# A whole fp32 copy of two kept products beside their high and low parts, in a hybrid recurrent and attention layer

## The chip, the cores and the metric

The kernel runs on one core of a Trainium2 chip. The metric is the time of the whole program on that core in microseconds (us), smaller is better. Engines are named as in the profile: PE multiplies matrices, DVE and ACT are the vector and the scalar engine, SP issues the transfers, POOL does next to nothing here.

## What is computed

One decoder layer over 2048 tokens of 1024 features, all in fp32. What matters here is its middle: the tokens attend to 256 fixed memory tokens in four heads. The reference, cut to that:

```python
h = rms_norm(x, xa_norm_g[l])
m = rms_norm(mem, mem_norm_g[l])
q = (h @ w_q[l]).reshape(bsz, s, XA_HEADS, XA_HD)
k, v = jnp.split(m @ w_kv[l], 2, axis=-1)
scores = jnp.einsum("bshd,bmhd->bhsm", q, k) * (XA_HD ** -0.5)
p = jax.nn.softmax(scores, axis=-1)
o = jnp.einsum("bhsm,bmhd->bshd", p, v).reshape(bsz, s, d)
x = x + o @ w_o[l]
```

Ahead of it stands a mixer (a gated linear recurrence beside a convolution module with 31 taps, one input and one output projection), behind it a gated feed-forward part with a short convolution, and a last norm.

## The kernel before

**Two parts per operand.** PE multiplies rounded fp32 (`fp32r`). To keep precision each operand is split into a high part `h` (ACT copies it with rounding) and a low part `l` (DVE subtracts the high part from the source); a product is three matmuls: high by high, high by low, low by high (`mm3`).

**Folded attention weights.** Since memory and weights are fixed over the tokens, the kernel first makes two weights from them: `A`, 1024 by 1024, which takes normed tokens straight to scores (from the keys and `w_q`), and `VO`, which takes probabilities straight to the output (from the values and `w_o`). `memory_a` makes `A`: 16 banks of PSUM of 128 by 512, each with two blocks of 128 by 256. `memory_vo` makes `VO`: 16 banks of 128 by 512. Each bank is split into a pair (`ah`, `al`, or `voh`, `vol`), and `keep` stores both parts to DRAM (tensors `A2`, `VO2`), from where they are fetched again whenever they are used.

**Tokens in four groups of 512.** Groups 0 and 1 go through the attention one after the other. Groups 2 and 3 go as a pair, by Strassen's scheme with seven products for eight. For it `Folds.prepare` makes four combinations (`T1` to `T4`) of the blocks of each weight: `w_out`, `A` and `VO`. It takes every block through `Folds.block`: that of `w_out` is fetched whole from the input; for `A` and `VO` both parts are fetched and DVE adds them (`wd<-wh,wl`). That is 16 blocks for `A` and 16 for `VO`. The combinations go to DRAM and are split when they are used. The feed-forward part follows in two halves and takes the last 1,400 us or so.

**Order of the work.** The code writes tasks (mixers `m`, attentions `a`, `mem_a`, `mem_vo`, `fold` and others) which are stepped by a clock of PE's planned work. The instructions that they write are then put in order by a list scheduler (`Program.schedule`): each has a due time that follows from the place of its users on PE, an estimated duration and an engine, and each engine takes the one due first of those that are ready; 84 slots of 128 by 512 fp32 in SBUF and 8 banks of PSUM are given out in the order of the program. The schedule fixes the order on each engine, and the tile framework adds the semaphores. All instructions are thus recorded at line 399, which is why the profile is read by tiles. All large transfers go through one queue, SP's, in order.

**Names.** `raw` is a weight as fetched, `wh`/`wl` its parts; `mt` the normed memory, `kvh`/`kvl` keys or values, `qth`/`qtl` the turned `w_q`; `x` a token tile, turned on PE by products with the identity (`ps<-ident,x`) and split to `xh`/`xl`; `cb`, `conv` the 31-tap convolution, whose 30 steps are DVE's `conv<-cb,v,conv`; `hid` and `X` operands of the feed-forward part.

Of the kernel before, what the change touches and what calls it, by code (L numbers as in the profile page):

```python
# [11 lines left out]
F32 = mybir.dt.float32  # L12
F32R = mybir.dt.float32r
AF = mybir.ActivationFunctionType
ALU = mybir.AluOpType
# [407 lines left out]
def hybrid_layer(  # L423
# [17 lines left out]
    pr = Program(nc, place)  # L441
# [4 lines left out]
    def V(name, *a, **k):  # L446
        pr.do("DVE", name, *a, **k)

    def ACT(out, in_, func, **k):
        pr.do("ACT", "activation", out, in_, func, **k)  # L450
# [4 lines left out]
    def transpose(o, in_, idn):  # L455
        pr.do("PE", "transpose", o, in_, idn)
# [8 lines left out]
    def ps():  # L465
        return pr.new("ps", name="ps")

    def tmp(name="tmp"):
        return pr.new("S", name=name)

    def rnd(name, shape=None):
        return pr.new("S", shape, F32R, name)

    def pair(name, shape=None):
        return rnd(name + "h", shape), rnd(name + "l", shape)
# [48 lines left out]
    def small(w):  # L524
        at = n_small[0]
        n_small[0] += w
        return Buf(None, (P, w), smalls[:, at : at + w])
# [49 lines left out]
    def split(src, hi, lo):  # L577
        ACT(hi[:], src, AF.Copy)
        V("tensor_tensor", lo[:], src, hi[:].f32(), op=ALU.subtract)
# [26 lines left out]
    class Kept:  # L606


        def __init__(self, name, n, dtype=F32R):
            self.t = drp.tile([n * P, TT], F32, name=name)  # L610
            self.tok = {}
            self.dtype, self.name, self.n = dtype, name, n
# [9 lines left out]
        def get(self, i, shape=None, name=None):  # L622
            b = pr.new("S", shape, self.dtype, name or self.name)
            pr.dma((b[:] if shape is None else flat(b)).f32(), self.at(i), reads=[self.tok[i]])
            return b
# [6 lines left out]
    def raw_rows(w, r0):  # L632
        st = pr.new("W", (P, D), name="raw")
        pr.dma(st[:], w[r0 : r0 + P, :])
        return st
# [41 lines left out]
    class Rows:  # L677


        def __init__(self, w, name, n, uses):  # L680
            self.w, self.kept, self.uses, self.seen = w, Kept(name, n * 4), uses, {}

        def get(self, k, half):
            base = (k * 2 + half) * 2
# [240 lines left out]
    def kv(c0):  # L925

        hi, lo = pair("kv")
        pp = [ps(), ps()]
        for kq in range(2):
            st = raw_cols(w_kv[0], c0, kq)  # L930
            for f in range(2):
                with together():
                    for k in range(KQ):
                        sl = slice((k % 2) * M, (k % 2 + 1) * M)
                        matmul(pp[f][:, :M], st[:, k, f * P : (f + 1) * P], mt[kq * 2 + k // 2][:, sl], start=kq + k == 0, stop=kq == 1 and k == KQ - 1)
            yield 0
        for f in range(2):
            fs = slice(f * M, (f + 1) * M)
            ACT(hi[:, fs], pp[f][:, :M], AF.Copy)
            V("tensor_tensor", lo[:, fs], pp[f][:, :M], hi[:, fs].f32(), op=ALU.subtract)  # L940
        return hi, lo

    def keep(rows, k, half, cols, src):

        base = (k * 2 + half) * 2
        for i in range(2):
            tok = rows.kept.tok.setdefault(base + i, Buf(None, (1,)))
            pr.dma(rows.kept.at(base + i)[:, cols], src[i].f32(), writes=[tok], join=True)

    def memory_a():  # L950
        pr.first = True
        xs = []
        for mb in range(2):
            parts = []
            ssp = small(2)
            for half in range(2):
                t = tmp("mem")
                pr.dma(t[:], mem[0, mb * P : (mb + 1) * P, half * TT : (half + 1) * TT])
                ACT(junk[:], t[:], AF.Square, accum_out=ssp[:, half : half + 1])
                parts.append(t)  # L960
            r = small(1)
            V("tensor_tensor", r[:], ssp[:, 0:1], ssp[:, 1:2], op=ALU.add)
            ACT(r[:], r[:], AF.Sqrt, bias=eps[:], scale=1.0 / D)
            V("reciprocal", r[:], r[:])
            for t in parts:
                ACT(t[:], t[:], AF.Copy, scale=r[:, 0:1])
            xs.append(parts)
        for k2 in range(NK // 2):
            t = tmp("mt")
            p = ps()  # L970
            with together():
                for kk in range(2):
                    k = 2 * k2 + kk
                    for mb in range(2):
                        transpose(p[:, kk * M + mb * P : kk * M + (mb + 1) * P], xs[mb][k // 4][:, (k % 4) * P : (k % 4 + 1) * P], ident[:])
            for kk in range(2):
                sl = slice(kk * M, (kk + 1) * M)
                ACT(t[:, sl], p[:, sl], AF.Copy, scale=vec["v1024"][:, 2 * k2 + kk, G_MEM : G_MEM + 1])
            mt.append(t)
        pr.first = False  # L980
        yield MEM_WAIT
        def operands(h):
            kk = yield from kv(h * M)
            yield 0

            qt = []
            for kq in range(2):
                st = raw_cols(w_q[0], h * M, kq)
                for db in range(2):
                    p = ps()  # L990
                    with together():
                        for j in range(KQ):
                            transpose(p[:, j * P : (j + 1) * P], st[:, j, db * P : (db + 1) * P], ident[:])
                    hi, lo = pair("qt")
                    split(p[:], hi, lo)
                    qt.append((hi, lo))
            yield 1
            return kk, qt

        nxt = yield from operands(0)  # L1000
        for h in range(4):
            (kh, kl), qt = nxt
            if h < 3:
                nxt = yield from operands(h + 1)
            for k2 in range(NK // 2):
                p = ps()
                with together():
                    for kk in range(2):
                        k = 2 * k2 + kk
                        for db in range(2):  # L1010
                            hi, lo = qt[(k // KQ) * 2 + db]
                            cs = slice((k % KQ) * P, (k % KQ + 1) * P)
                            ks = slice(db * M, (db + 1) * M)
                            mm3(p[:, kk * M : (kk + 1) * M], hi[:, cs], lo[:, cs], kh[:, ks], kl[:, ks], db == 0, db == 1)
                t = pair("a")
                split(p[:], *t)
                for kk in range(2):
                    keep(A_rows, 2 * k2 + kk, h // 2, slice((h % 2) * M, (h % 2 + 1) * M), [b[:, kk * M : (kk + 1) * M] for b in t])
                yield 0
            yield 0  # L1020

    def memory_vo():
        yield mem_a
        yield VO_LATE
        for h in range(4):
            vh, vl = yield from kv(D + h * M)
            yield 1
            pp = [ps() for _ in range(4)]
            for db in range(2):
                st = raw_rows(w_o[0], h * M + db * P)  # L1030
                ww = []
                for half in range(2):
                    hi, lo = pair("w")
                    split(st[:, half * TT : (half + 1) * TT], hi, lo)
                    ww.append((hi, lo))
                for i, p in enumerate(pp):
                    mb, (wh, wl) = i // 2, ww[i % 2]
                    vs = slice(db * M + mb * P, db * M + (mb + 1) * P)
                    with together():
                        mm3(p[:], vh[:, vs], vl[:, vs], wh[:], wl[:], db == 0, db == 1)  # L1040
                    if i % 2:
                        yield 0
            for i, p in enumerate(pp):
                t = pair("vo")
                split(p[:], *t)
                keep(VO_rows, h * 2 + i // 2, i % 2, slice(0, TT), [b[:] for b in t])


# [589 lines left out]
    class Folds:  # L1638
# [5 lines left out]
        def block(self, k, half):  # L1644
            if self.rows.w is not None:
                t = tmp("wd")
                pr.dma(t[:], self.rows.w[k * P : (k + 1) * P, half * TT : (half + 1) * TT])
                return t
            hi, lo = self.rows.get(k, half)
            t = tmp("wd")  # L1650
            V("tensor_tensor", t[:], hi[:].f32(), lo[:].f32(), op=ALU.add)
            return t

        def prepare(self, wait):
            for i in range(KH):
# [348 lines left out]
    m, n, a = mixers, normeds, attends  # L2004
# [44 lines left out]
```

## Time and profile before

| | us |
|---|---|
| median of three runs | 2402.87 |
| lowest and highest run | 2400.91, 2404.35 |
| the profiled execution, its own time | 2401.64 |
| its span in the trace | 2399.8 |
| PE, DVE, ACT busy in it | 2385.4, 2034.9, 1319.6 |

The granted clock of PE was 0.999 over the span. 604.56 MB were moved by DMA, 252 GB/s on average. PE's rows overlap: a matmul of 128 by 512 is shown with some 390 ns, and the next one starts 226 to 227 ns later. So a share of busy time says only that PE never stopped; where it waits is read from the waits and from the distance of starts. The same holds in a lesser degree for DVE and ACT, whose rows overlap by about 0.1 us. In the trace an fp32 product that is not rounded (`ps<-mt,raw`) has two rows where the program has one instruction.

### The profile page before, as it was taken

The page shows a single profiled execution, that of the slowest core. Times are in us where ns is not written, and L with a number is a line of the kernel's source. Part 1 is how long each engine was busy: PE and PEld are TensorE (multiplying, and loading weights), DVE is VectorE, ACT ScalarE, POOL GpSimd, SP SyncE. Part 2 cuts the span into 40 slices and gives each one's busy share as a digit, 9 for nine tenths or more (in the row PEclk, how much of TensorE's full clock was granted, in tenths as well). Part 3 has the DMA queues.
Part 4 walks back from the last instruction along what each step waited for, and adds up shares of the span by engine and source line. Part 5 has one row for each costly group of instructions (what it writes and reads, how often), then busy time and mean ns, then how long its engine had stood idle before and what let it go on. Part 6 is the DMA issues. An engine that isn't in the chain of part 4 may idle for free.

```text
span 2399.8 us, 33427 instructions
## 1 busy us (share of the span) xinstructions
PE 2385.4 (99%) x10940; PEld 1977.0 (82%) x10940; DVE 2034.9 (85%) x3353; ACT 1319.6 (55%) x2380; POOL 0.7 (0%) x6
## 2 busy tenths in 40 slices
PE   9999999999999999999999999999999999999998
PEld 8798888888887888888888888888888888888887
DVE  6999995299899869879999887988988896777787
ACT  7782676357557778695555555554555541222333
POOL 0000000000000000000000000000000000000000
PEclk9999999999999999999999999999999999999999
DMA  9688788775878988787766544556565599887986
GB/s 308 220 297 314 241 298 301 255 263 175 289 261 272 322 275 273 277 284 268 253 231 205 199 171 158 174 177 211 192 215 199 184 308 321 283 280 253 315 299 255
DMA packets 364434, 604.56 MB, mean 252 GB/s; under 512 B 35371, under 2 KB 117547, under 8 KB 364260
## 3 DMA queue, kind: packets, MB, share of 16 engines
q1 hardware_dynamic: 364108, 602.16, 73.3%
q8 instruction: 86, 1.41, 0.2%
q14 instruction: 88, 0.72, 0.1%
q10 hardware_dynamic: 152, 0.28, 0.0%
HBM read 409.36 MB, written 192.94 MB: 251 GB/s over the span
## 4 chain that ended last, share of the span: by engine, by line
PE 84%; DVE 9%; ACT 3%; DMA 2%; issue 1%; SPq 0%; DVEq 0%; ACTq 0%
PE ps L399 84%; DVE conv L399 4%; DMA h<-hid 1%; DMA wl<-w_down 1%; ACT L399 1%; DVE wl L399 1%; DVE hidl L399 0%; DVE s L399 0%; DVE acc L399 0%; ACT gate L399 0%; DVE al L399 0%; ACT junk L399 0%; DMA wl<-w_in 0%; DVE xc L399 0%; DVE xl L399 0%
## 5 line engine op out<-in xcount | busy, mean ns | idle before, releaser
L399 PE MATMUL ps<-Xh,wh 128*128 128x512 f32 x1344 | 523.5, 390 | 0.7 <-ACT u L399 0.7
L399 PE MATMUL ps<-Xh,wl 128*128 128x512 f32 x1344 | 523.4, 389 | 0.7 <-DVE wl L399 0.5
L399 PE MATMUL ps<-Xl,wh 128*128 128x512 f32 x1344 | 523.2, 389 | 0.0
L399 PE MATMUL ps<-wh,hidl 128*128 128x512 f32 x960 | 374.4, 390 | 1.0 <-DVE hidl L399 1.0
L399 PE MATMUL ps<-wh,hidh 128*128 128x512 f32 x960 | 374.5, 390 | 0.8 <-ACT hidh L399 0.8
L399 PE MATMUL ps<-wl,hidh 128*128 128x512 f32 x960 | 373.8, 389 | 0.0
L399 DVE SCALAR_TENSOR_TENSOR conv<-cb,v,conv 128x512 f32<-128x512 f32 x480 | 337.1, 755 | 2.2 <-ACT conv L399 1.4
L399 PEld LDWEIGHTS ps<-Xh,wl 128*128 128x128 f32 x1344 | 252.4, 188 | 53.6 <-DVE wl L399 1.5
L399 PEld LDWEIGHTS ps<-Xh,wh 128*128 128x128 f32 x1344 | 252.4, 188 | 53.1 <-ACT u L399 1.1
L399 PEld LDWEIGHTS ps<-Xl,wh 128*128 128x128 f32 x1344 | 252.4, 188 | 52.4
L399 ACT ACTIVATE hidh<-s 128x512 fp32r<-128x512 f32 x186 | 113.8, 631 | 271.1 <-DVE s L399 232.6
L399 PEld LDWEIGHTS ps<-wh,hidl 128*128 128x128 f32 x960 | 180.3, 188 | 40.2 <-DVE hidl L399 3.1
L399 PEld LDWEIGHTS ps<-wh,hidh 128*128 128x128 f32 x960 | 180.3, 188 | 38.3 <-ACT hidh L399 1.3
L399 PEld LDWEIGHTS ps<-wl,hidh 128*128 128x128 f32 x960 | 180.3, 188 | 37.1
L399 PE MATMUL ps<-xh,wh 128*128 128x512 f32 x512 | 204.6, 400 | 0.5 <-DVE vol L399 0.5
L399 PE MATMUL ps<-xh,wl 128*128 128x512 f32 x512 | 200.4, 391 | 0.0
L399 PE MATMUL ps<-xl,wh 128*128 128x512 f32 x512 | 200.1, 391 | 0.0
L399 ACT ACTIVATE wh<-s 128x512 fp32r<-128x512 f32 x192 | 119.5, 629 | 116.7 <-DVE s L399 82.0
L399 ACT ACTIVATE wh<-raw 128x512 fp32r<-128x512 f32 (+2 forms) x214 | 127.9, 613 | 54.2 <-PE ps L399 22.7
L399 ACT ACTIVATE u<-ps 128x512 f32<-128x512 f32 x144 | 85.7, 595 | 129.1 <-PE ps L399 128.2
L399 DVE TENSOR_TENSOR wl<-raw,wh 128x512 fp32r<-128x512 f32 (+2 forms) x214 | 141.5, 675 | 14.7 <-ACT wh L399 13.7
L399 DVE TENSOR_TENSOR acc<-acc,ps 128x512 f32<-128x512 f32 (+1 forms) x157 | 103.4, 682 | 59.2 <-PE ps L399 55.3
(241 smaller groups left out, 4029.9 us busy)
## 6 DMA issues: line engine op xcount, KB each, us to landing
raw<-in_w_up_dram SPq DMA_DIRECT2D x96, 512.0 KB
wh<-w_down SPq DMA_DIRECT2D x156, 256.0 KB
wl<-w_down SPq DMA_DIRECT2D x156, 256.0 KB
w_down<-wh SPq DMA_DIRECT2D x144, 256.0 KB
w_down<-wl SPq DMA_DIRECT2D x144, 256.0 KB
h<-hid SPq DMA_DIRECT2D x120, 256.0 KB
wh<-w_in SPq DMA_DIRECT2D x96, 256.0 KB
wl<-w_in SPq DMA_DIRECT2D x96, 256.0 KB
```

The source lines that it names most:

```text
L399: getattr(e, name)(*[resolve(a) for a in args], **{k: resolve(a) for k, a in kw.items()})
```

## The change

A third tensor of whole fp32 values is kept for `A` and for `VO` (`A2w`, `VO2w`). `split_kept` makes it: after the split ACT copies the same bank of PSUM once more, unrounded, to a tile `aw` or `vow`, and `keep` stores that too. `Folds.block` then fetches the whole block instead of both parts, and DVE's addition is gone.

```diff
         def __init__(self, w, name, n, uses):
             self.w, self.kept, self.uses, self.seen = w, Kept(name, n * 4), uses, {}
+            self.whole = None if w is not None else Kept(name + "w", n * 2, F32)
...
             pr.dma(rows.kept.at(base + i)[:, cols], src[i].f32(), writes=[tok], join=True)
+        tok = rows.whole.tok.setdefault(k * 2 + half, Buf(None, (1,)))
+        pr.dma(rows.whole.at(k * 2 + half)[:, cols], src[2], writes=[tok], join=True)
+
+    def split_kept(name, p):
+        t = *pair(name), tmp(name + "w")
+        split(p[:], *t[:2])
+        ACT(t[2][:], p[:], AF.Copy)
+        return t
...
-                t = pair("a")
-                split(p[:], *t)
+                t = split_kept("a", p)
...
-                t = pair("vo")
-                split(p[:], *t)
+                t = split_kept("vo", p)
...
-            hi, lo = self.rows.get(k, half)
-            t = tmp("wd")
-            V("tensor_tensor", t[:], hi[:].f32(), lo[:].f32(), op=ALU.add)
-            return t
+            return self.rows.whole.get(k * 2 + half, None, "wd")
```

In numbers of instructions: ACT has 16 `aw<-ps` and 16 `vow<-ps` more and three loads of its function tables fewer (81 to 78); DVE has 32 `wd<-wh,wl` fewer; SP has 32 stores `A2w<-aw` of 128 KB and 16 stores `VO2w<-vow` of 256 KB more, 32 fetches `wd` of 256 KB more, and 64 fetches of parts fewer. PE's instructions are the same 10,790. The scheduler puts the rest in a new order. PE's first difference is its 690th instruction, and from about its 4,520th on, which is all of the feed-forward part, its order is as before. On DVE, ACT and SP the order differs in pieces between about 120 and 1,200 us of the trace of before, and hardly after that.

Three places show what moved. The first is PE at the end of `memory_a`, where the second group of tokens is turned and its mixer begins. Before:

```order
L399 MATMUL ps<-mt,raw 128x256 x8
L399 MATMUL ps<-ident,x 128x128 x24
L399 MATMUL ps<-mt,raw 128x256 x4
L399 MATMUL ps<-ident,x 128x128 x8
L399 MATMUL ps<-xh,wh 128x512
L399 MATMUL ps<-xl,wh 128x512
L399 MATMUL ps<-xh,wl 128x512
```

Now:

```order
L399 MATMUL ps<-mt,raw 128x256 x8
L399 MATMUL ps<-ident,x 128x128 x16
L399 MATMUL ps<-mt,raw 128x256 x4
L399 MATMUL ps<-ident,x 128x128 x4
L399 MATMUL ps<-mt,raw 128x256 x4
L399 MATMUL ps<-ident,x 128x128 x12
L399 MATMUL ps<-wh,kvh 128x512
L399 MATMUL ps<-wl,kvh 128x512
L399 MATMUL ps<-wh,kvl 128x512
```

Four more products for the values (`ps<-mt,raw`) and then the first 24 products for `VO` now stand between the turned tokens and the mixer's first product; before, they stood among the mixer's products.

The second place is DVE over the same stretch, from the last subtractions of `A` on. Before:

```order
L399 TENSOR_TENSOR al<-ps,ah 128x512
L399 TENSOR_TENSOR wl<-raw,wh 128x512 x2
L399 SCALAR_TENSOR_TENSOR conv<-cb,v_99,conv 128x512
L399 TENSOR_TENSOR wl<-raw,wh 128x512 x2
L399 SCALAR_TENSOR_TENSOR xl<-ps,v_98,xh 128x512 x5
L399 TENSOR_TENSOR kvl<-ps,kvh 128x256
L399 SCALAR_TENSOR_TENSOR xl<-ps,v_98,xh 128x512 x3
```

Now:

```order
L399 SCALAR_TENSOR_TENSOR conv<-cb,v_101,conv 128x512 x3
L399 TENSOR_TENSOR smalls<-smalls 128x4
L399 SCALAR_TENSOR_TENSOR conv<-cb,v_101,conv 128x512 x2
L399 RECIPROCAL smalls<-smalls 128x4
L399 TENSOR_TENSOR al<-ps,ah 128x512 x2
L399 SCALAR_TENSOR_TENSOR conv<-cb,v_101,conv 128x512 x9
L399 SCALAR_TENSOR_TENSOR xl<-ps,v_100,xh 128x512 x2
L399 TENSOR_TENSOR wl<-raw,wh 128x512 x2
L399 TENSOR_TENSOR kvl<-ps,kvh 128x256
L399 TENSOR_TENSOR wl<-raw,wh 128x512
L399 SCALAR_TENSOR_TENSOR xl<-ps,v_100,xh 128x512
```

Nine steps of the convolution now stand between the last `al` and the first `xl`, where one stood, and the sums of the tokens' norm (`smalls`) stand shortly ahead of the last `al` instead of ahead of the last head. Between the first and the last `al` there are three more steps of the convolution than before (30 to 27), and 68 instructions in all to 65.

The third is ACT at the last head of `A`, with the engines that each row waits for. Before:

```order
L399 ACTIVATE x<-x,smalls 128x512
L399 ACTIVATE ah<-ps 128x512 [waits PE_49]
L399 ACTIVATE x<-x,smalls 128x512
L399 ACTIVATE x<-x,smalls 128x512 [waits DMAHW4_49]
L399 ACTIVATE ah<-ps 128x512 [waits PE_49]
```

Now:

```order
L399 ACTIVATE aw<-ps 128x512 [waits DVE_49]
L399 ACTIVATE ah<-ps 128x512 [waits PE_49]
L399 ACTIVATE smalls<-smalls,eps 128x4 [waits DVE_49]
L399 ACTIVATE aw<-ps 128x512
L399 ACTIVATE ah<-ps 128x512 [waits PE_49]
L399 ACTIVATE aw<-ps 128x512
L399 ACTIVATE x<-x,smalls 128x512 [waits DVE_49]
L399 ACTIVATE x<-x,smalls 128x512 x6
L399 ACTIVATE x<-x,smalls 128x512 [waits Activation_49]
```

Before, the eight token tiles were scaled (`x<-x,smalls`) among the copies of `A`; now all eight stand behind the last of them. Six of the 16 `aw` rows wait for DVE.

## The prediction

> **What bounds the kernel now.** I read the page first, then PE's waits, then the stretches.
>
> ```profile
> span 2399.8 us, 33427 instructions
> PE 2385.4 (99%) x10940; PEld 1977.0 (82%) x10940; DVE 2034.9 (85%) x3353; ACT 1319.6 (55%) x2380; POOL 0.7 (0%) x6
> PE 84%; DVE 9%; ACT 3%; DMA 2%; issue 1%; SPq 0%; DVEq 0%; ACTq 0%
> ```
>
> PE is busy in all but 14.4 us, and the chain that ended last is PE's for 84%. A change that leaves PE's work alone can give back only its waits. These are all that the view of waits lists for PE:
>
> ```profile
> PE ps L399 <- DMA raw<-in_w_in_dram: 1.6, 1, 1.6
> PE ps L399 <- POOL ident masks.py:199: 1.4, 1, 1.4
> PE ps L399 <- DVE hidl L399: 1.0, 2, 0.6
> PE ps L399 <- DVE xl L399: 0.8, 2, 0.5
> PE ps L399 <- ACT hidh L399: 0.8, 1, 0.8
> PE ps L399 <- ACT u L399: 0.7, 1, 0.7
> PE ps L399 <- DVE wl L399: 0.5, 1, 0.5
> PE ps L399 <- DVE vol L399: 0.5, 1, 0.5
> PE ps L399 <- ACT prob L399: 0.3, 1, 0.3
> ```
>
> The first two are the start, `xl` is there before the change sets in, and `hidl`, `hidh`, `u` and `wl` (3.0 us) lie behind 1,000 us, in the feed-forward part. In the stretch that is reordered only `vol` and `prob` remain, 0.8 us. In the chain told in order of time PE runs alone over long pieces:
>
> ```profile
> 265.09 450.67 PE ps L399 x2109
> 770.20 722.32 PE ps L399 x3302
> ```
>
> DVE's share lies ahead of the first, below 265 us, and between 716 and 770. There DVE hardly rests (columns: length; busy time and rows of PE, PEld, DVE, ACT, POOL; clock, DMA share, GB/s):
>
> ```profile
> 120.00:140.00 20.00, 20.00 (x123) 18.47 (x122) 19.97 (x34) 19.85 (x35) 0.00 (x0) 1.00 0.80 261
> 140.00:160.00 20.00, 20.00 (x144) 19.00 (x144) 20.00 (x35) 14.65 (x37) 0.00 (x0) 1.00 0.93 317
> 160.00:180.00 20.00, 20.00 (x139) 18.42 (x138) 20.00 (x34) 15.88 (x29) 0.00 (x0) 1.00 0.97 313
> 180.00:200.00 20.00, 20.00 (x90) 16.66 (x89) 19.54 (x30) 4.52 (x8) 0.00 (x0) 1.00 0.85 281
> 200.00:220.00 20.00, 20.00 (x91) 16.89 (x91) 19.86 (x32) 6.23 (x13) 0.00 (x0) 1.00 1.05 395
> 680.00:720.00 40.00, 40.00 (x180) 32.09 (x179) 39.48 (x64) 24.59 (x35) 0.00 (x0) 1.00 0.82 278
> 720.00:760.00 40.00, 39.74 (x195) 32.14 (x194) 39.55 (x65) 36.89 (x66) 0.00 (x0) 1.00 0.80 273
> ```
>
> From 120 to 180 us, where `A` is made, PE and DVE are full, DMA nearly, and ACT has 9.6 us left of 60. That is where the change adds. Where it removes, PE has next to no waits.
>
> **What it removes.** The additions, by the view of the tile `wd`:
>
> ```profile
> L399 DVE TENSOR_TENSOR wd<-wh,wl x32: 671/688/702, 611.4 to 965.8; 128x512 f32<-128x512 f32 x32
> ```
>
> 32 x 0.688 = 22.0 us of DVE, and 32 fetches of 256 KB (8.4 MB) out of that stretch. DVE is full in part of it (39.55 of 40 above), but PE's waits there sum to 0.3 us (`prob`). So 22 us of DVE are worth 0.3 us at most. The three table loads and the SBUF slots that come free end no wait of PE that the list shows. These I take at -0.3.
>
> **What it adds: 32 copies on ACT.** The nearest row is the first copy of the same banks, with the subtraction beside it:
>
> ```profile
> L399 ACT ACTIVATE ah<-ps x16: 577/597/648, 130.9 to 168.3; 128x512 fp32r<-128x512 f32 x16
> L399 DVE TENSOR_TENSOR al<-ps,ah x16: 684/698/706, 131.6 to 171.3; 128x512 fp32r<-128x512 f32 x16
> ```
>
> 16 copies at 0.597 us are 9.6 us of ACT between 131 and 170 us, just what it had left. The scheduler answers by moving the scaling of the second group's tokens behind the last copy and giving DVE convolution steps meanwhile. What that costs is read at the point where PE needs the tokens. Before:
>
> ```profile
> 168.14 3.62 PE L399 MATMUL ps<-mt,raw 128*128 128x256 f32 x16
> 171.59 2.78 PE L399 MATMUL ps<-ident,x 128*128 128x128 f32 x24
> 174.21 1.89 PE L399 MATMUL ps<-mt,raw 128*128 128x256 f32 x8
> 175.94 1.15 PE L399 MATMUL ps<-ident,x 128*128 128x128 f32 x8
> 177.09 0.50 PE L399 MATMUL ps<-xh,wh 128*128 128x512 f32 x1
> 163.00 1.42 DVE L399 SCALAR_TENSOR_TENSOR conv<-cb,v,conv 128x512 f32<-128x512 f32 x2
> 164.32 0.70 DVE L399 TENSOR_TENSOR al<-ps,ah 128x512 fp32r<-128x512 f32 x1
> 171.28 0.71 DVE L399 TENSOR_TENSOR al<-ps,ah 128x512 fp32r<-128x512 f32 x1
> 171.88 1.31 DVE L399 TENSOR_TENSOR wl<-raw,wh 128x512 fp32r<-128x512 f32 x2
> 173.09 0.77 DVE L399 SCALAR_TENSOR_TENSOR conv<-cb,v,conv 128x512 f32<-128x512 f32 x1
> 174.95 3.40 DVE L399 SCALAR_TENSOR_TENSOR xl<-ps,v,xh 128x512 fp32r<-128x512 f32 x5
> 178.24 0.44 DVE L399 TENSOR_TENSOR kvl<-ps,kvh 128x256 fp32r<-128x256 f32 x1
> 157.85 0.73 ACT L399 ACTIVATE x<-x,smalls 128x512 f32<-128x512 f32 x1 [0.78 <-DVE smalls L399]
> 161.74 1.36 ACT L399 ACTIVATE x<-x,smalls 128x512 f32<-128x512 f32 x2
> 162.97 0.62 ACT L399 ACTIVATE ah<-ps 128x512 fp32r<-128x512 f32 x1
> ```
>
> These are rows of PE, DVE and ACT with start and length. Distances of starts give the step of each form: `conv` (164.32 - 163.00)/2 = 0.66, `al` 171.88 - 171.28 = 0.60, `wl` (173.09 - 171.88)/2 = 0.61, `xl` (178.24 - 174.95)/5 = 0.66, a scaled token tile (162.97 - 161.74)/2 = 0.62; on PE a turned block (174.21 - 171.59)/24 = 0.109 and four `mt,raw` of the program (eight rows) 175.94 - 174.21 = 1.73.
>
> PE alone: it is free at 175.94 + 8 x 0.109 = 176.81 and starts the mixer at 177.09, a gap of 0.28. With four more `mt,raw` it would be ready for the first `VO` product at 178.54.
>
> DVE: since it is full, its order can be added up. Three more steps ahead of the last `al` put that at 171.28 + 3 x 0.66 = 173.26. Behind it come the `al` 0.60, nine `conv` 5.94, two `xl` 1.32, two `wl` 1.22 and `kvl` 0.44: 182.8 us. The `VO` products need that `kvl`, so PE is held 182.8 - 178.5 = 4.3 us.
>
> ACT and PE give nearly the same by another way. The reciprocal of the norm now stands just ahead of the last two `al`, at about 172.6; four scaled tiles take 4 x 0.62, so turning begins at 175.1 where PE was ready at 171.59: 3.5 us late. I take DVE's 4.3, less the old gap of 0.28: +4.0. Bounds: nothing, if the nine steps only fill time in which DVE would wait for ACT anyway and the transposes come no later; 7 us if ACT's late copies add their own 3.5 to part of it.
>
> Once PE is 4 us later, DVE is that much ahead, so the wait for `vol` at the next gates goes: -0.5. The sum is +4.0 - 0.5 - 0.3 = +3.2, against the profile's own time 2401.64 (span 2399.8): 2404.8. That execution lay 1.2 below the median of the three, so 2406.0. From 990 us on PE's order is the old one and I count nothing.
>
> **A rule of the skill against the change.** The subtraction `al` starts between 0.1 us (the first pair) and 2.4 us (the last) after the end of its `ah`, and a third read by ACT now stands between or behind. No row of before has one bank read three times. The Trainium skill, "PSUM — Partial Sum Buffer", section "PSUM bank collisions raise a hardware error", says that two engines must not touch one bank at once, reads included, and that the compiler's scheduler orders them by a dependency. By that rule the copy and the subtraction take turns, as the waits for DVE at six `aw` rows suggest, and the sum grows to that of the first rival; without it the copy runs beside the subtraction and the sum stays.
>
> **The rivals.**
>
> *The turns at the bank decide, slower.* Where the copy stands ahead, the subtraction waits for up to one ACT step more (0.5 us); ten of the 16 `aw` rows do not wait for DVE, so up to 5 us on a full DVE. The six others hold ACT for up to 2.4 us each. For it: no slack on either engine. Against: where the subtraction comes later than that the copy fits between, as in the pair quoted above, whose `ah` ends at 162.97 + 0.62 and whose `al` starts at 164.32. From the point where it delays `kvl` past 182.8 it counts in full; at 4 us the time is 2410.
>
> *The stores crowd the loads, slower.* 4.2 MB of `A2w` in 62 us at 315 GB/s are 13 us of transfer where the shares above leave 5 us in 140:200. Loads could come 8 us late. Against: 395 GB/s were reached in 200:220, and the mixer's weights are needed later now, by about 4.3 + 1.7 + 24 x 0.227 = 11 us. If half is uncovered: 2410.
>
> *The freed DVE counts, faster.* Had DVE between 600 and 970 us been holding back what the feed-forward part starts from, the waits `hidl`, `hidh`, `u`, `wl` (3.0) go with `vol` and `prob` (0.8), and no hold appears at the tokens: 2399. For: DVE full at 680:760. Against: PE runs from 770 to 1,492 us without a step to another engine in the chain, so nothing made before can still be late there.
>
> *It does nothing that counts.* The hold is covered, the 0.8 us come: 2402.
>
> **How the numbers follow.** Forecast 45%, turns at the bank 23%, stores 8%, freed DVE 12%, nothing 12%. About 0.2%, 4.8 us, is what a measurement of this kernel can tell from no change: below 2398.1 is faster, above 2407.7 slower. The forecast's own range is 2403 to 2409; of its 45% I count 32% as no change and 13% as slower. With both slower rivals slower has 44%; no change 32 + 12 = 44%; faster 12%. The time is the forecast's, 2406; the range 2399 to 2413 takes in the rivals' prices and leaves out the ends of each.
>
> **What would show it.** Right: PE stands 3 to 5 us in front of the first turned tokens or the first `ps<-wh,kvh` between 170 and 185 us, released by ACT's `x` or DVE's `kvl`; the waits of PE behind 1,400 us look as before; between 600 and 970 us DVE has 22 us less and PE the same. Turns at the bank: `al` regularly released by `aw`, `aw` by `al`, DVE no longer 20 of 20. Stores: PE or ACT released by `wh<-w_in` or `raw`. Wrong: no wait of over 2 us near 180 us, or a new one where the order is the old one.

## The result, and the profile after

The change makes the kernel slower: 2429.49 us (median of four runs, 2423.92 to 2431.25) against 2402.70 (2400.91 to 2404.35) for the kernel before on the same chip, a ratio of 1.0108 with a 95% interval of 1.0095 to 1.012. That is 26.8 us more; forecast were 2406 and a range up to 2413. The profiled execution took 2431.25 us, with a span of 2429.5. One execution of e7 below took 8,595 us and counts as slow; it is left out of the time given there.

The head of the page of the kernel after:

```profile
span 2429.5 us, 33456 instructions
PE 2396.6 (99%) x10940; PEld 1980.2 (82%) x10940; DVE 2017.8 (83%) x3321; ACT 1329.2 (55%) x2409; POOL 0.7 (0%) x6
```

DVE has 17 us less of busy time, PE the same instructions and 11 us more of busy time, and the span has grown by 29.7: 18 us of new standing (span less busy time, 32.9 against 14.4) and 11 us of longer running. A stretch in which PE waits is called a stand below. These lead the view of PE's waits; they were absent or small before (`in_w_in` 1.6, `xl` 0.8):

```profile
PE ps L399 <- ACT aw L399: 6.3, 1, 6.3
PE ps L399 <- DVE xl L399: 4.5, 6, 1.7
PE ps L399 <- DMA raw<-in_w_kv_dram: 4.5, 2, 3.3
PE ps L399 <- DMA raw<-in_w_in_dram: 3.2, 1, 3.2
PE ps L399 <- ACT diagh L399: 1.7, 1, 1.7
```

The wait for `in_w_in` lies in the first 60 us, ahead of the change, and differs between the kernels that do the same there (1.6 in before, 3.3 in e3). Where the others lie, by the starts of PE's n-th row in both traces (the order differs in places, so only the level counts, not a single row): after is 0.8 us behind at the 600th row, 2.3 at the 750th, 11.1 at the 900th (172 us of before), 17.8 at the 1050th, 25.7 at the 1950th (399 us), 27.0 at the 3000th (618 us) and 29.0 at the 10,500th (2292 us). Nearly all of it is lost between 140 and 425 us. The windows of that stretch, with the columns of the prediction's fence:

```profile
140.00:160.00 20.00, 18.85 (x128) 17.20 (x127) 20.00 (x34) 13.83 (x29) 0.00 (x0) 1.00 0.85 270
160.00:180.00 20.00, 13.73 (x97) 13.01 (x96) 17.71 (x30) 16.56 (x39) 0.00 (x0) 0.86 0.94 291
200.00:220.00 20.00, 16.70 (x59) 12.69 (x58) 18.18 (x26) 2.58 (x5) 0.00 (x0) 0.83 1.03 351
220.00:240.00 20.00, 20.00 (x90) 16.70 (x90) 14.37 (x24) 6.31 (x15) 0.00 (x0) 1.00 1.05 402
400.00:420.00 20.00, 16.59 (x86) 13.62 (x86) 11.33 (x23) 17.28 (x40) 0.00 (x0) 0.92 0.99 348
```

PE has holes at 160:180, 200:220 and 400:420, and there the granted clock falls to 0.86, 0.83 and 0.92 (and, running on, to 0.97 in 180:200 and 0.91 in 420:440); in before it was 1.00 in all of these windows. PE's rows in order of time show both:

```profile
176.96 5.85 PE L399 MATMUL ps<-mt,raw 128*128 128x256 f32 x16 [6.27 <-ACT aw L399]
...
212.86 6.67 PE L399 MATMUL ps<-mt,raw 128*128 128x256 f32 x16 [3.30 <-DMA raw<-in_w_kv_dram]
...
413.68 0.66 PE L399 MATMUL ps<-ident,x 128*128 128x128 f32 x4 [0.57 <-DVE xl L399]
415.44 0.66 PE L399 MATMUL ps<-ident,x 128*128 128x128 f32 x4 [1.11 <-DVE xl L399]
417.82 1.09 PE L399 MATMUL ps<-ident,prob 128*128 128x128 f32 x4 [1.73 <-DVE xl L399]
418.56 0.78 PE L399 MATMUL ps<-wh,xah 128*128 128x512 f32 x1
419.14 0.63 PE L399 MATMUL ps<-wl,xah 128*128 128x512 f32 x1
419.56 0.63 PE L399 MATMUL ps<-wh,xal 128*128 128x512 f32 x1
```

The same 16 rows of `mt,raw` took 3.62 us in before. So the first stand costs 6.27 and then 2.2 more, the second 3.30 and then 3.0; behind three short ones near 415 us, 11 rows start 0.425 us apart (419.14 to 419.56, and so on to 423.40) in place of 0.227, another 2.2. Some 7 us of the loss are PE running at about half its rate after a stand. The Trainium skill, "TensorE: Matmul & The Clock Gate", section "What's actually happening", says that a gate grants half the clock after an idle window of about 3.4 us and the full clock again after about that long a busy one; the trace agrees for the stands of 3.30 and 6.27 us, behind which the clock is 0.50 (windows 214:218 and 176:180). Near 415 us it goes further than that sentence: no stand there is longer than 1.73 us, and the clock is 0.50 from 418 to 422 all the same.

What the first stand waited for is read in three more views. In the chain that ended last, two loads of after now stand that are not in that of before:

```profile
161.96 4.59 DMA x<-in_x_dram
...
208.62 4.11 DMA raw<-in_w_kv_dram
```

ACT, in order of time, waits for the first of them with the copies of `A` queued behind (in brackets the idle time and what ended it):

```profile
162.77 0.64 ACT L399 ACTIVATE junk<-x 128x512 f32<-128x512 f32 x1 [1.52 <-DMA x<-in_x_dram]
...
166.62 0.63 ACT L399 ACTIVATE junk<-x 128x512 f32<-128x512 f32 x1 [1.18 <-DMA x<-in_x_dram]
...
175.30 0.58 ACT L399 ACTIVATE aw<-ps 128x512 f32<-128x512 f32 x1
175.78 0.59 ACT L399 ACTIVATE ah<-ps 128x512 fp32r<-128x512 f32 x1
176.25 0.60 ACT L399 ACTIVATE aw<-ps 128x512 f32<-128x512 f32 x1
```

The stand had a second cause of the same length. The products in front of which PE stood also needed the weights `raw` that SP issues at 172.80 below; by the trace's semaphores they landed at 176.83, and the last copy `aw` ended at 176.85. Either alone would have held PE as long; the view names the later one.

And SP, which issues these loads. Before (start, duration, count):

```profile
140.08 0.41 SPq L399 DMA_DIRECT2D raw<-in_w_kv_dram  x1
140.58 2.87 SPq L399 DMA_DIRECT2D x<-in_x_dram  x6
...
157.97 0.92 SPq L399 DMA_DIRECT2D A<-ah  x2
158.98 0.90 SPq L399 DMA_DIRECT2D A<-al  x2
159.97 0.42 SPq L399 DMA_DIRECT2D raw<-in_w_kv_dram  x1
```

After:

```profile
158.42 0.89 SPq L399 DMA_DIRECT2D A2w<-aw  x2
159.36 0.45 SPq L399 DMA_DIRECT2D x<-in_x_dram  x1
159.91 0.88 SPq L399 DMA_DIRECT2D A<-al  x2
160.88 0.97 SPq L399 DMA_DIRECT2D A<-ah  x2
161.96 0.40 SPq L399 DMA_DIRECT2D x<-in_x_dram  x1
162.45 0.38 SPq L399 DMA_DIRECT2D A2w<-aw  x1
162.92 2.87 SPq L399 DMA_DIRECT2D x<-in_x_dram  x6
...
172.80 1.00 SPq L399 DMA_DIRECT2D raw<-in_w_kv_dram  x2
```

A single issue of these rows takes 0.38 to 0.45 us of SP with some 0.05 to 0.1 between (a row of several has its pauses in), and SP issues in order. The first of the eight token loads has gone from 140.6 to 159.4, the weights of the first values from 160.0 to 172.8. For the weights the added stores are all that is new in the queue: 165 transfers stood ahead of them in before and 181 now, the 16 more being `A2w`. For the tokens they are not: 138 stood ahead of the first load and now 159, of which 12 are `A2w` and six are stores of `A` that stood behind it before, so the planner has moved it too. The experiments ask whether it is these stores, and by their bytes, their number, or the new order that comes with them.

### The profile page after: what moved, and what is told of

Read it like the earlier page. It is cut to its first block, busy times and chain, and to the rows that moved or that the text cites. A ratio compares the mean times of both kernels' runs of the same rounds, so it can differ in the third digit from the quotient of the medians.

```text
span 2429.5 us, 33456 instructions
## 1 busy us (share of the span) xinstructions
PE 2396.6 (99%) x10940; PEld 1980.2 (82%) x10940; DVE 2017.8 (83%) x3321; ACT 1329.2 (55%) x2409; POOL 0.7 (0%) x6
## 4 chain that ended last, share of the span: by engine, by line
PE 85%; DVE 8%; DMA 4%; ACT 2%; issue 1%; SPq 0%; DVEq 0%; ACTq 0%
PE ps L399 85%; DVE conv L399 3%; DMA wl<-w_down 1%; DMA h<-hid 1%; DVE s L399 1%; DVE hidl L399 1%; DVE wl L399 1%; DVE acc L399 0%; DVE xc L399 0%; ACT L399 0%; ACT junk L399 0%; SPq L399 0%; DVE gate L399 0%; DMA w_in<-wl 0%; ACT hidh L399 0%
```

## The experiments

The planner is the list scheduler that puts the instructions in order. The excerpts of code show the lines that matter; the rest of an edit is left out. All times are medians of a few runs on the chip; "+" is the difference from the kernel before, run beside it on the same chip, and the interval is that of the ratio to it. None of the kernels is faster than the kernel before beyond what can be measured.

### Taking the change apart

**e1, the copies alone.** The change without its 48 stores, the additions kept:

```diff
-        pr.dma(rows.whole.at(k * 2 + half)[:, cols], src[2], writes=[tok], join=True)
...
-            return self.rows.whole.get(k * 2 + half, None, "wd")
+            hi, lo = self.rows.get(k, half)
+            t = tmp("wd")
+            V("tensor_tensor", t[:], hi[:].f32(), lo[:].f32(), op=ALU.add)
+            return t
```

> The 32 extra copies stay on ACT, their stores go, and the additions on DVE stay as they were before (the copied tiles are read by nothing). In the changed kernel PE loses about 1.6 us at 152, 8.7 at 170 to 183, 6.6 at 209 to 219, 1.8 at 311 and 6.1 at 412 to 423. If the third read of each bank (banks held longer, subtractions that wait for the copy) makes the loss at 170 to 183, that loss stays and the others go: 2410 to 2414. If the stores on the queue make it (token loads late, ACT held by them): 2402 to 2405. If any new order of the schedule costs this much: 2415 or more, with losses at other places.

Measured: 2404.84, +1.8 (1.0008, 0.9999 to 1.0018). The copies with two readers of each bank, and the order that the planner makes for them, cost next to nothing.

**e2, the stores alone.** No copy, the additions kept; the high part is stored a second time:

```diff
+        pr.dma(rows.whole.at(k * 2 + half)[:, cols], src[0].f32(), writes=[tok], join=True)
```

> The 48 extra stores stay, but they store the high part a second time, so that no copy is made and each bank is read twice as before; the additions stay. If the stores make the losses (loads of w_kv and of tokens late at 152, 170 and 209): 2412 to 2425, with PE waiting for raw<-in_w_kv and ACT waiting for x<-in_x. If the copies make them: 2402 to 2406.

Measured: 2421.10, +18.0 (1.0074, 1.0059 to 1.0089). Two thirds of the loss come with the stores.

**e3, the additions alone taken away.** In the kernel before `Folds.block` fetches the high part and adds nothing:

```diff
+            n = self.rows.seen[k, half] = self.rows.seen.get((k, half), 0) + 1
+            return self.rows.kept.get((k * 2 + half) * 2, None, "wd")
```

> Only what the change removes: a block of A or VO is fetched by its high part alone and nothing is added (the low parts are left out of the combinations), so DVE has 32 additions fewer and the queue 32 fetches fewer, and nothing is added anywhere. If the freed DVE is worth next to nothing: 2401 to 2403. If it is worth something that the change hides: 2396 to 2399.

Measured: 2403.47 (1.0002, 0.9993 to 1.0011). The 22 us of DVE and the fetches that the change removes are worth nothing; so is the reordering that e1 and e3 bring, though over a hundred rows stand elsewhere on PE in both.

**e4, the whole copy first.** The whole change, with one reader of the bank; both parts are made from the copy in SBUF:

```diff
-        split(p[:], *t[:2])
         ACT(t[2][:], p[:], AF.Copy)
+        split(t[2][:], *t[:2])
```

> All of the change, but the whole copy is taken first and both parts are made from it, so each bank of PSUM has one reader and comes free after one ACT step. Same number of copies, stores, fetches. If the third read of the bank is the cause at 170 to 183: that loss goes, 2414 to 2421. If ACT's added time and the stores are: 2425 to 2432 as the change itself.

Measured: 2418.20, +15 (1.0063, 1.0048 to 1.0078): 11 us back, as the expectation had it for the third read of the bank. But with e1 at +1.8 that read costs little by itself. What e4 gains it gains beside the stores and in another order (over 300 of PE's rows stand elsewhere); the runs do not part the two.

**e5, a quarter of the bytes**, **e6, the stores of `A` only**, **e7, those of `VO` only**, **e8, the stores from POOL's queue**, each from e2:

```diff
e5  +        pr.dma(rows.whole.at(k * 2 + half)[:32, cols], src[0][:32].f32(), writes=[tok], join=True)
e6  +        if rows is not A_rows:
    +            return
e7  +        if rows is not VO_rows:
    +            return
e8  +        pr.dma(rows.whole.at(k * 2 + half)[:, cols], src[0].f32(), writes=[tok], join=True, by="Pool")
```

> As the run of the stores alone (2421), with the same 48 stores, but each takes 32 of the 128 partitions: as many transfers on SP, a quarter of the bytes (2.1 MB; three quarters of the copy are left out). If the bytes cost the time (the engines of DMA are full at 200 to 260 us): 2403 to 2408. If the number of transfers in the one queue does (turns, waits in order): 2415 to 2422.

> Stores alone again, for A only: 32 stores of 128 KB between 131 and 195 us. In the run with both, PE lost about 8 us up to 200 us and 8 at 264. If the stores of A make the late loads of w_kv and w_o, the first 8 stay: 2409 to 2413, and if the wait at 264 is what is left of the same delay, 2418 or more.

> Stores alone, for VO only: 16 stores of 256 KB between 196 and 380 us. If only the full DMA at 200 to 260 us counts, this alone shows the 8 us at 264: 2409 to 2413. If A's stores come first in the chain: 2403 to 2406, nothing of note.

> Stores alone, all 48, issued by POOL, which has nothing else to do, so that SP's queue holds the same transfers as before. The bytes are the same. If the place of the stores in SP's queue is the cause: 2402 to 2408. If the bytes are: 2415 to 2425, the loads still late.

Measured: e5 2414.19 (1.0049, 1.0034 to 1.0064), 7 better than e2 and between its two ranges; e6 2410.39 (1.0035, 1.0022 to 1.0048); e7 2403.79 (1.0005, 0.9995 to 1.0014); e8 2408.83 (1.0028, 1.0018 to 1.0038), 12 better than e2. The stores of `A` are the costly ones; `VO`'s stores alone find room (`A` 8, `VO` 2, both together 18, so the two do not add). The issuing queue seems to matter most, and the bytes too; but each of these kernels has an order of its own from the planner, and that is what the later runs hold fast.

### Three guesses at SP's queue

**e9, stores later.** From e2, `A`'s added stores go into the queue two banks later, with their data ready:

```diff
+        args = rows.whole.at(k * 2 + half)[:, cols], src[0].f32(), [tok]
+        if rows is A_rows:
+            held.append(args)
+        else:
+            late(0, args)
...
                 t = split_kept("a", p)
+                late(2, after=[t[0]])
```

> Stores alone (2421.1), with each store of A's third tensor put into SP's queue two banks later, so that its data lie ready when its turn comes; as many transfers, the same bytes, the same queue, and the loads ahead or behind by a few places only. Theory 'issue': between 153 and 177 us SP issues back to back, one transfer in some 0.5 us (0.41 to 0.49 for the issue itself), so 32 more of them keep it for 16 us; waits do not matter: 2417 to 2424. Rival 'wait': SP stands in front of stores whose data are not there, and the loads behind it stand too: 2408 to 2413. Theory 'bytes' (DMA shared by more traffic): 2421.

Measured: 2418.23 (1.0065, 1.005 to 1.008), 2 to 3 better than e2. SP standing in front of stores that are not ready is not the main thing.

**e10, wide stores.** From e2, one 256 KB store for the two of 128 KB of each bank (`dst` takes both blocks of 128 rows):

```diff
+        pr.dma(dst, src[:, :].f32().split2(2), writes=toks, join=True)
```

> Stores alone, with the two 128 KB stores of each of A's banks to the third tensor issued as one of 256 KB: 16 transfers fewer, the same bytes. 'Issue': 8 us of SP less, so about half of what moving the stores to another queue gave (12): 2413 to 2417. 'Wait': the wide store waits for the same data: 2419 to 2423. 'Bytes': 2421.

Measured: 2420.41 (1.0075, 1.006 to 1.009): no gain in the end, which "issue" had not expected. The trace tells why. PE's 1000th row is 2.3 us late where in e2 it was 7.1, so the stretch of `A` did get its loads in time; but then PE stands 5.7 us near 265 us, released by `xh`, and the rows behind that start within a microsecond of e2's.

**e11, the whole change with its 48 stores from POOL's queue**, and **e12, the whole change with the whole copy first and all stores of `A` wide** (48 where the change has 96, and before 64):

```diff
e11 +        pr.dma(rows.whole.at(k * 2 + half)[:, cols], src[2], writes=[tok], join=True, by="Pool")
e12 +                for i in range(2):
    +                    keep_wide(A_rows.kept, k2, h // 2 * 2 + i, 4, cs, t[i])
    +                keep_wide(A_rows.whole, k2, h // 2, 2, cs, t[2])
```

> The whole change, with the 48 stores of whole values issued by POOL in place of SP. 'Issue' and 'wait': the loads come in time again, 2429.5 - 12 = 2417, range 2413 to 2420; what is left above 2402.9 is the traffic (7), the copies (2) and the readers of the bank. 'Bytes' alone: 2427 to 2430.

> The whole change, the whole copy made first and both parts made from it, and all stores of A issued as one transfer for a bank and part: 48 in place of the change's 96 (before: 64). 'Issue': less SP time than before the change, so 2429.5 - 11 (whole copy first) - 12 = 2406, range 2403 to 2411. 'Bytes' and 'wait': 2415 to 2419. Neither expects less than 2401, since the missing additions were worth nothing.

Measured: e11 2412.50 (1.0038, 1.0024 to 1.0052), e12 2416.91 (1.006, 1.0045 to 1.0075). Moving 48 transfers to another queue, with the same work otherwise, takes 17 of the change's 27 us away, more than in e2; the planner's order changes with it (some 350 of PE's rows stand elsewhere). e12 has fewer stores of `A` than the kernel before and still loses 15, hardly less than e4; "issue" had expected 2403 to 2411 for it. There the number of transfers is not what is left. PE's 1200th row is 4.6 us late in it, where the change has 17.9, and the 1950th 11.1, so most is lost behind the stretch of `A`.

### The order held fast

In all these kernels the planner makes a new order. e13 to e16 are planned as the kernel before, and the added work is hung on existing steps afterwards: PE, DVE and the transfers of before keep their order row for row (ACT's too, but for the added copies). What e16 leaves out: the additions stay, and the stores take the high part, so that no store waits for a copy.

```diff
e13 +            if i == 0:
    +                pr.ops[-1].calls.append(("dma_start", (), dict(out=rows.whole.at(k * 2 + half)[:, cols], in_=src[0][:].f32())))
e14 the same with [:32, cols] and src[0][:32]
e15 the same, issued by POOL
e16 e13, and behind each copy of a high part:
    +        pr.ops[-2].calls.append(("activation", (w[:], p[:], AF.Copy), {}))
```

> The 48 stores of stores alone (e2, 2421.1), each put behind the store of the same high part in SP's queue after the order has been fixed: PE, DVE, ACT and all other transfers keep exactly the order of the kernel before; added are only 48 transfers and 8.4 MB in SP's queue. Theory 'queue': the loads behind the stores come late and PE waits for them as in e2: 2414 to 2422. Theory 'order': the stores themselves are nearly free and the planner's new order, made for transfers that it believes to issue in 0.1 us, costs the rest: 2403 to 2408.

> As e13_same_order, with 32 of the 128 partitions stored: as many transfers, a quarter of the bytes. If the number of transfers in SP's queue counts: as e13, within 2 us. If the bytes count: at most a third of what e13 loses.

> As e13_same_order, with the 48 stores issued by POOL, which does next to nothing else. If a place in SP's queue counts: 2403 to 2406. If the bytes count, wherever they are issued: as e13, within 2 us. (With the planner's own order this move gave 12 of 18.)

> As e13_same_order, and ACT makes the 32 whole copies too, each right behind the copy of the high part; they go to one spare tile that nobody reads. All work that the change adds, in the order of before. Copies were worth 1.8 in their own order, so e13 + 2 if they and the stores add up; e13 + 5 to 9 if ACT, full from 120 to 180 us, holds up the scaling of the tokens as well as the stores do.

Measured: e13 2416.05 (1.0057, 1.004 to 1.0073), e14 2414.32 (1.0051, 1.0036 to 1.0066), e15 2408.87 (1.0025, 1.0015 to 1.0036), e16 2414.52 (1.0051, 1.0036 to 1.0066).

So 48 more transfers in SP's queue cost 13.4 us with nothing else moved. A quarter of the bytes changes that by 1.7, within what the runs scatter; the same transfers from POOL cost 6.2, so about half is the place in SP's queue. What the other half is, when POOL issues them, stays open. In e15's trace SP's transfers have the order of before, and yet the load of 159.97 goes out at 163.68 and ACT waits 6.1 us for two loads of `w_o`, for which it does not wait in before; the share of the DMA engines in 140:160 is 1.01 (0.93 in before). That points to the shared engines; a quarter of the bytes from POOL would tell, and no run tries it. The copies on top add nothing that the medians show. Two views of e13 say how it happens, PE's waits and SP in order of time:

```profile
PE ps L399 <- DMA raw<-in_w_kv_dram: 4.3, 3, 2.2
...
PE ps L399 <- DVE xl L399: 2.0, 4, 0.8
PE ps L399 <- DVE al L399: 1.7, 1, 1.7
```

```profile
165.17 1.38 SPq L399 DMA_DIRECT2D A2w<-ah  x1
166.64 0.87 SPq L399 DMA_DIRECT2D A<-al  x2
167.61 0.40 SPq L399 DMA_DIRECT2D raw<-in_w_kv_dram  x1
168.11 0.49 SPq L399 DMA_DIRECT2D A<-ah  x1
168.66 0.42 SPq L399 DMA_DIRECT2D A2w<-ah  x1
169.13 0.49 SPq L399 DMA_DIRECT2D A<-ah  x1
169.66 0.51 SPq L399 DMA_DIRECT2D A2w<-ah  x1
170.27 0.95 SPq L399 DMA_DIRECT2D A<-al  x2
171.32 0.40 SPq L399 DMA_DIRECT2D raw<-in_w_kv_dram  x1
```

SP issues back to back; the load that went out at 159.97 in before goes out at 167.61, in the same place of the order but for the 16 added stores ahead of it, 0.48 us for each. The Trainium skill, "DMA: Bandwidth & Descriptors", section "Issuing engines are not separate DMA queues", says that issuing from several engines only saves the time that it takes to initiate a transfer, which is usually small beside the transfer. Beside the time from issue to landing it is small here too (4.11 us for the `raw` in the chain above). Beside what a transfer takes of the shared engines it is not: 0.40 to 0.51 us a piece, where 128 KB at the 351 GB/s of window 200:220 take 0.37.

**e17, the whole change with the planner's figure mended, and e18, the kernel before with the same.** The planner reckons 0.1 us for an issue:

```diff
-ISSUE = dict(SP=0.1, ACT=0.3, Pool=1.0)
+ISSUE = dict(SP=0.48, ACT=0.3, Pool=1.0)
```

> The whole change, with the planner told that SP takes 0.48 us to issue a transfer, as the traces show, where it reckons 0.1; the work is the change's, only the order is made anew. If the 14 us that the change loses beyond the same work in the held order (e16, 2414.5) come from an order that was planned for loads that come too early: 2408 to 2418. If they come from the change's order for another reason (copies on a full ACT): 2424 to 2432.

> The kernel before with the same figure in its planner, as the comparison for e17. PE waits for 7.6 us in all, 1.6 of it for a load: 2400 to 2406.

Measured: e17 2420.93 (1.0074, 1.0059 to 1.0089), e18 2401.95 (0.9996, 0.9986 to 1.0006). 8.6 us of the change's loss go, which is between the two ranges, and the two stands of 170 and 210 us with them: PE's 1200th row is 1.7 us late where it was 17.9. But some 10 us are lost again at 265 us. DVE there, in order of time, and ACT:

```profile
258.12 6.06 DVE L399 SCALAR_TENSOR_TENSOR conv<-cb,v,conv 128x512 f32<-128x512 f32 x9
264.08 0.76 DVE L399 SCALAR_TENSOR_TENSOR xc<-z,v,xc 128x512 f32<-128x512 f32 x1
```

```profile
258.01 0.80 ACT L399 ACTIVATE xc<-z,v 128x512 f32<-128x512 f32 x1
...
267.52 0.63 ACT L399 ACTIVATE xh<-xc 128x512 fp32r<-128x512 f32 x1 [4.63 <-DVE xc L399]
```

The first `xc` is ready for DVE at 258.01 + 0.80 and is taken up at 264.08, behind nine convolution steps. In PE's waits that is now the longest:

```profile
PE ps L399 <- ACT xh L399: 5.5, 1, 5.5
```

The same nine steps stand ahead of it in e2 and e10. In before there were three:

```profile
256.44 2.10 DVE L399 SCALAR_TENSOR_TENSOR conv<-cb,v,conv 128x512 f32<-128x512 f32 x3
```

That is order, not transfers: a planned place on an engine that is full.

## Why the prediction was wrong

**Right: what bounds the kernel, and what the removal is worth.** Removal was put at -0.3; in e3 it is worth nothing that can be measured. The rival of the freed DVE (12%) falls with it. The wait for `vol` is gone from PE's list, as forecast. Behind 1,000 us, where nothing was counted, about 2 us were lost.

**Near its place, wrong in its cause: the hold near 180 us.** Forecast were 4.3 us, added up along a full DVE, with bounds of 0 and 7, in front of the turned tokens or of the first product for `VO`. PE stood 6.27 us in front of the `mt,raw` ahead of both, up to 176.96, and was held by the last copy `aw` and, just as long, by the load of `w_kv`. That the size lies within the bounds is luck. DVE was not full there (17.71 of 20, where the sum had reckoned with 20 of 20), because its work had come late: ACT had waited 2.7 us (1.6 in before) for token tiles whose first was issued 18.8 us later than before. Only a part of these 18.8 is the added stores in the queue. In e13, where eight of them stand ahead of that load and the rest is in the order of before, it goes out 3.0 later (143.61). The rest is the planner's new place for it, and what SP waited for ahead of it.

**The step that failed: the stores.** The sum of the forecast (+4.0 - 0.5 - 0.3) has no term for the transfers; it takes each of them at its old time. They come in only as a rival: "The stores crowd the loads" had 8% and a price of 2410. It weighed bytes, 13 us of transfer against 5 us of room, and asked whether the mixer's weights would still come in time. Three things were wrong in it. In SP's queue the bytes count for little (e14: 1.7 of 13.4), and the place in that in-order queue counts (e15: 7 of 13.4; what makes the other 6 is not shown). The loads that came late were others, the tokens and the weights of the values, which stand in that queue right among the stores. And it was priced as half of 8 us; with the order held the stores alone cost 13.4 (e13). SP was named in the prediction nowhere but in the share of the chain, which read 0% for it: before the change it had room (by its rows 10 to 16 us of issues in each 20 from 140 to 220), and nobody waited for it. The sign that the text gave for this rival, PE or ACT released by `raw`, is what the trace shows.

**The half rate after a stand was not in the sum.** The two stands of over 3 us cost 2.2 and 3.0 us on top and the three short ones 2.2, about 7 in all.

**The turns at the bank (23%)** did not decide. `al` was released by `aw` three times for 2.6 us in all; the copies alone cost 1.8 (e1), and nothing in the held order (e16 against e13). That one reader gives 11 us back (e4) is not explained by these; it comes with another order, and its cause stays open.

**What of the 27 us is shown.** Stores in SP's queue with the order held 13.4; copies and removal about nothing. The other 13 to 15, by what is left and by the change against e16, come with the new order and with what e16 leaves out: stores that wait for the copies. Part goes when the planner reckons 0.48 us for an issue (e17, 8.6). The nine steps of 265 us are not a part: the change itself loses nothing there (17.9 us late at PE's 1200th and at its 1320th row, 238 and 264 us of before). A part may be this place of ACT in the change, where two copies for `VO` stand ahead of the scaled tokens whose `xl` PE then waits for near 415 us:

```profile
397.54 1.28 ACT L399 ACTIVATE vow<-ps 128x512 f32<-128x512 f32 x2
398.71 3.78 ACT L399 ACTIVATE x<-x,smalls 128x512 f32<-128x512 f32 x6
```

That place was read from the trace and not tried by itself. The parts do not add up cleanly, since a loss at 170 us and one at 265 us hide one another: e10 and e17 removed the first and paid at the second.

## What to carry to other kernels

Count the transfers that a change adds, not only their bytes: SP, which issues in order, took about half a microsecond for each here, and the loads behind them in its queue went out that much later (7.6 us behind 16 stores in e13). Where a planner decides the order, separate the added work from the new order by hanging the work on the old order; the two cost about the same here (13.4 in e13, and 13 to 15 more in the change). And where PE is 99% busy, price a stand with its restart.

## What was not expected of the hardware

A stand of 3.30 us already halved PE's rate behind it (16 rows in 6.67 us, not 3.62), and so did three short ones of 0.57, 1.11 and 1.73 us within 5 us. By the clock records of the trace the half clock lasted 6.8 us each time (from 174.51, 212.05 and 416.85), and PE had stood 3.4, 2.5 and 2.1 us of the 3.4 us before it set in: a stand did not have to fill them. And an issue on SP cost much the same whatever it moved: in the rows of after, pauses within a row included, 0.45 us for 128 KB (two `A2w` in 0.89), 0.48 for 256 KB (six `x` in 2.87), 0.50 for 512 KB (two `raw` in 1.00).
